# Output projection's weights scaled and split on GpSimd instead of ScalarE and VectorE, in a one-core decoder layer

## The chip, the cores and the metric

The kernel runs on one core of a Trainium2 chip. The metric is the device time of one execution in microseconds (us), taken as the median of three runs. A core has a matrix engine (TensorE, PE in the profile, with its weight loads as PEld), VectorE (DVE), ScalarE (ACT), GpSimd (POOL) and SyncE (SP). Each engine works through its own list of instructions in order, and waits at an instruction until what it needs has arrived. All transfers to and from memory in this kernel are issued from SP's list, in order as well.

## The reference, cut to what matters

One layer over 2048 tokens of width 1024. Four mixers of width 256 each make a part of `ycat`; each part is normalised; one product with `w_out` follows, and the result is added to `x`:

```python
y_a = _chunked_sgu(a_u, a_v, sgu_w[l], sgu_b[l])
y_b = _multiscale_pool(b_in, pool_w[l], pool_scale[l])
y_c = _swa_sink_attention(c_q, c_k, c_v, swa_sinks[l], rel_bias)
y_d = _stick_breaking_attention(d_q, d_k, d_v)
ycat = jnp.stack([y_a, y_b, y_c, y_d], axis=2)
ycat = _rmsnorm(ycat, mix_out_gain[l].reshape(N_MIXERS, GROUP_WIDTH))
x = x + ycat.reshape(B, S, D_MODEL) @ w_out[l]
h = _rmsnorm(x, norm_ffn[l])
gate, up = jnp.split(h @ w_gate_up[l], 2, axis=-1)
x = x + (jax.nn.silu(gate) * up) @ w_down[l]
```

## The kernel before, in words

Every product is made of three passes of TensorE on split operands: a number is rounded to a high part, and the low part is what the rounding left over. So each weight matrix is loaded, scaled, rounded (high part) and subtracted (low part) before it can be used. For `w_out` the function `load_wo` does this. It takes the matrix in eight pieces k = 0 to 7 of 128 rows. Piece k is loaded into a buffer `oraw` (128x1024, 512 KB; two such buffers, so the load of piece k waits until piece k-2 has been read), and gives two pairs `wo` (128x512 high and low each), one for each half n of the output's columns. `gout` holds the gains by which the rows are scaled.

The program has three stages that matter here. In the first, `stick` works through eight chunks of the stick-breaking attention (pair 0 and 1, c = 0 to 3). Each of its steps goes around the engines: `z` (PE), two sigmoids `tfix` and `s` (ACT), a running product `pr` (DVE), `s` times `pr` (line 343: DVE, but GpSimd for i = 3 of the last chunk, by `ON_G`), transposes `tr` (PE), `wt` high (ACT) and low (DVE), and the product `acc` (PE). The last chunk ends with `accs`, `yp` and `ysb`, and SP stores `ysb` into `yd`, two stores.

`mixer_c` is the sliding-window attention, in eight steps s of 256 tokens (`swa`). Step s loads `kr` and, for two groups, `qr`; GpSimd rounds `qr` into `cq` (line 460) and subtracts (line 461); PE makes the logits `z` (line 468); then come a maximum, exponentials on ACT (line 490), transposes `trc` (line 504), copies of these into the buffer `block` (line 506, ACT), the products `o` (line 510) and a store into `yd`. Its steps run beside the last chunk of `stick`, and then beside the output projection.

In `last()` the pieces of `w_out` are prepared beside the last chunk of `stick` and the first steps of `swa`. Then comes `out_proj`, over 16 row blocks b of 128 tokens: load `y` from `yd`; four sums of squares `junk` (ACT); `orr` (a power, on GpSimd, line 149); scale `y`; transpose to `yT` (high on ACT, low on DVE); for each half 8 x 3 products `ops` with `wo` (lines 728 to 730, 48 for a row block); add to `xres`. `finish` normalises the result, transposes it (line 690) and stores it; its power `fr` is also on GpSimd. After that come the feed-forward stages, to the end of the program.

Which instruction stands where in each engine's list is set by the framework's scheduling at build time (`schedule_with_timeline_sim`), from the order in the code, the data that each needs, the buffers and its own costs for the operations. So a change of one function moves others' instructions too. On the chip the lists are fixed.

Of the kernel before, what the change touches and what calls it, by code (L numbers as in the profile page):

```python
# [9 lines left out]
F32 = mybir.dt.float32  # L10
F32R = mybir.dt.float32r
AF = mybir.ActivationFunctionType
ALU = mybir.AluOpType
# [103 lines left out]
def _build(nc, tc, A, top):  # L117
    V, S, G = nc.vector, nc.scalar, nc.gpsimd

    def load(out, in_):  # L120
        nc.sync.dma_start(out, in_)
# [40 lines left out]
    def fetch(pool, f):  # L162

        tag, n = ("k4", 16) if f else ("raw", 2)
        raw = [pool.tile([P, 2, CH], F32, name="fraw", tag=tag, bufs=n) for _ in range(2)]
        for u in range(2):
            load(raw[u], A["w_gu"][f, :, u].rearrange("p (a k) m -> p a (k m)", a=2))
        return raw

    with ExitStack() as ph1:  # L170
# [462 lines left out]
        def load_wo():  # L633

            gout = ring[0].tile([P, KT], F32, name="gout", bufs=1)
            load(gout, A["mix_out_gain"])
            for k in range(KT):
                raw = ring[0].tile([P, 2, CH], F32, name="oraw", tag="raw", bufs=2)
                load(raw, A["w_out"][k * P:(k + 1) * P, :].rearrange("p (n c) -> p n c", n=2))
                wo.append([ring[0].tile([P, 2, CH], F32R, name="wo", tag="k4") for _ in range(2)])  # L640
                for n, w in enumerate(wo[-1]):
                    S.activation(w[:, 0], raw[:, n], AF.Copy, scale=gout[:, k:k + 1])
                    V.scalar_tensor_tensor(w[:, 1], raw[:, n], gout[:, k:k + 1], w[:, 0].bitcast(F32),
                                           op0=ALU.mult, op1=ALU.subtract)
                yield

        def split_T(src, dst, banks=(("tr", 2), ("tr", 2))):
# [267 lines left out]
        def last():  # L915

            yield from upto(99)
            fps.close()
            ring.append(top.enter_context(tc.tile_pool(name="ring", bufs=16, side="right", reuse_waits="tile")))
            for _ in load_wo():  # L920
                yield 0.5
            while done[0] < 2:
                yield next(sw[0])
# [39 lines left out]
    with ExitStack() as ph4:  # L963
# [149 lines left out]
        for blk in range(T // TB):  # L1113
            for f in range(NF):
                raw = first if blk + f == 0 else fetch(ring, f)
# [18 lines left out]
```

## Time and profile before

| | us |
|---|---|
| median of 3 runs (2399.28 to 2400.28) | 2400.15 |
| the profiled execution's own time | 2402.21 |
| its span, from first to last instruction | 2400.5 |
| PE busy in the span | 2271.7 (95%) |
| DVE busy | 1505.8 (63%) |
| ACT busy | 1024.8 (43%) |
| POOL busy | 278.8 (12%) |

The profiled execution was 2.06 us above the median, and 1.71 us of it lie outside the span. Busy shares are means over the whole program; the stage in question is less than a tenth of it. A row of the timeline gives the start in us from the span's beginning, the duration of the group in us, engine, line, operation, output and inputs, the number of instructions (x1, x2), and in brackets the idle time before it with what ended it. PEclk is the granted TensorE clock as a share of 2.4 GHz.

### The profile page before, as it was taken

How to read it: one execution, taken by the hardware profiler on the slowest of the kernel's cores; microseconds unless marked ns; L12 is line 12 of the kernel's file. 1: busy time of each engine (PE TensorE's matmuls, PEld its weight loads, DVE VectorE, ACT ScalarE, POOL GpSimd, SP SyncE). 2: the span in 40 equal slices, each digit the busy share in tenths (PEclk: the TensorE clock that was granted, in tenths of full speed). 3: DMA queues.
4: the chain of work that ended last, by engine and by line, in shares of the span. 5: the costliest groups of instructions: out<-in, count | busy, mean ns of one | idle time of the engine just before them, and what ended most of it. 6: DMA issues, size and time to landing. Idle time of an engine off the chain costs nothing.

```text
span 2400.5 us, 31011 instructions
## 1 busy us (share of the span) xinstructions
PE 2271.7 (95%) x11432; PEld 1915.6 (80%) x11432; DVE 1505.8 (63%) x2467; ACT 1024.8 (43%) x2176; POOL 278.8 (12%) x356
## 2 busy tenths in 40 slices
PE   6999999998977899989999999999999999999998
PEld 6989888887865787768888888888888888888886
DVE  4356989887675455567666666644576666653443
ACT  5556656664455243343333333533333333333332
POOL 4222423441122120100000000000000000000000
PEclk9999999998977999999999999999999999999999
DMA  7534322333532245753222223665432222234553
GB/s 278 190 130 171 139 89 88 106 103 112 192 105 91 100 139 162 234 186 98 91 92 80 79 79 125 200 201 168 146 104 84 79 86 89 87 107 141 186 174 123
DMA packets 141001, 314.05 MB, mean 131 GB/s; under 512 B 12688, under 2 KB 68400, under 8 KB 134704
## 3 DMA queue, kind: packets, MB, share of 16 engines
q1 hardware_dynamic: 140848, 312.06, 38.8%
q8 instruction: 90, 1.47, 0.2%
q14 instruction: 63, 0.52, 0.1%
HBM read 229.44 MB, written 82.58 MB: 130 GB/s over the span
## 4 chain that ended last, share of the span: by engine, by line
PE 73%; DMA 10%; DVE 8%; ACT 4%; issue 3%; POOL 2%; SPq 1%; DVEq 0%; POOLq 0%; ACTq 0%
PE dn L1081 20%; PE gb L1025 15%; PE gc L1025 10%; PE ga L1025 10%; DVE pr L338 2%; PE ops L728 2%; PE ops L730 2%; PE ops L729 2%; DMA y<-yd 1%; DVE s L343 1%; DMA qr<-cd 1%; DMA xt<-in_x 1%; PE ps L277 1%; PE ps L278 1%; PE ps L279 1%
## 5 line engine op out<-in xcount | busy, mean ns | idle before, releaser
L1081 PE MATMUL dn<-wd,act 128*128 128x512 f32 x2112 | 479.5, 389 | 0.0
L1081 PEld LDWEIGHTS dn<-wd,act 128*128 128x128 f32 x2112 | 396.5, 188 | 82.4
L1025 PE MATMUL gb<-T,fw 128*128 128x512 f32 x1584 | 388.2, 394 | 0.0
L1025 PEld LDWEIGHTS gb<-T,fw 128*128 128x128 f32 x1584 | 297.5, 188 | 68.5
L1025 PE MATMUL ga<-B,fw 128*128 128x512 f32 x1056 | 259.5, 394 | 0.0
L1012 ACT CAST fw<-fsum 128x512 fp32r<-128x512 f32 x176 | 108.4, 619 | 308.4 <-DVE fsum L1008 162.3
L1025 PEld LDWEIGHTS ga<-B,fw 128*128 128x128 f32 x1056 | 198.6, 188 | 45.9
L975 DVE TENSOR_TENSOR wd<-wr,wd 128x512 fp32r<-128x512 f32 x176 | 115.2, 689 | 186.4 <-ACT wd L1075 186.2
L1075 ACT CAST wd<-wr 128x512 fp32r<-128x512 f32 x176 | 102.0, 619 | 236.5 <-DMA wr<-in_w_down 208.8
L149 POOL TENSOR_TENSOR fr<-rs_t,mhalf 128x1 f32<-128x1 f32 x32 | 21.5, 674 | 1433.1 <-DVE rs_t L148 1428.2
L975 DVE TENSOR_TENSOR fw<-fsum,fw 128x512 fp32r<-128x512 f32 x176 | 120.9, 690 | 36.4 <-ACT fw L1012 36.0
L1025 PE MATMUL gc<-T,fw 128*128 128x512 f32 x528 | 131.6, 397 | 5.8 <-DVE T L975 5.8
L338 DVE TENSOR_TENSOR_SCAN pr<-tfix,cr 128x513 f32<-128x513 f32 x96 | 126.1, 1323 | 11.4 <-ACT tfix L329 11.1
L1025 PE MATMUL gc<-B,fw 128*128 128x512 f32 x528 | 128.0, 391 | 0.0
L1025 PEld LDWEIGHTS gc<-T,fw 128*128 128x128 f32 x528 | 100.6, 191 | 28.7 <-DVE T L975 6.2
L728 PE MATMUL ops<-wo,yT 128*128 128x512 f32 x256 | 105.7, 413 | 11.5 <-ACT yT L656 10.8
L1025 PEld LDWEIGHTS gc<-B,fw 128*128 128x128 f32 x528 | 99.2, 188 | 21.7
L343 DVE TENSOR_TENSOR s<-s,pr 128x512 f32<-128x512 f32 (+3 forms) x152 | 107.9, 717 | 10.8 <-POOL s L335 4.5
L356 DVE TENSOR_TENSOR wt<-tr,wt 128x512 fp32r<-128x512 f32 (+3 forms) x160 | 94.1, 601 | 29.5 <-ACT wt L355 29.3
L1012 ACT CAST fw<-fraw 128x512 fp32r<-128x512 f32 x132 | 81.7, 621 | 66.9 <-DVE fw L975 32.4
L730 PE MATMUL ops<-wo,yT 128*128 128x512 f32 x256 | 102.7, 407 | 3.4 <-DVE yT L657 3.4
L729 PE MATMUL ops<-wo,yT 128*128 128x512 f32 x256 | 104.2, 408 | 0.0
(234 smaller groups left out, 4499.0 us busy)
## 6 DMA issues: line engine op xcount, KB each, us to landing
fraw<-in_w_gu SPq DMA_DIRECT2D x88, 512.0 KB
wr<-in_w_down SPq DMA_DIRECT2D x88, 512.0 KB
h<-hd SPq DMA_DIRECT2D x32, 1024.0 KB
actd<-up SPq DMA_DIRECT2D x88, 256.0 KB
ar<-actd SPq DMA_DIRECT2D x88, 256.0 KB
hd<-h SPq DMA_DIRECT2D x16, 1024.0 KB
xr<-in_xT SPq DMA_DIRECT2D x16, 512.0 KB
xt<-in_x SPq DMA_DIRECT2D x16, 512.0 KB
```

Of the source, the lines that this page charges most:

```text
L277: nc.tensor.matmul(o, hk[:, 0], w(k, 0), start=k == 0, stop=False)
L338: V.tensor_tensor_scan(pr[:, c0:][:, ::-1], t[:, c0:][:, ::-1], t[:, c0:][:, ::-1], carry[h][i], op0=ALU.mult, op1=ALU.bypass)
L343: (G if (4 * pair + c, i) in ON_G else V).tensor_tensor(w[:, c0:], w[:, c0:], pr[:, c0 + 1:], op=ALU.mult)
L356: V.tensor_tensor(wt[:, 1, r], tr[:, r], wt[:, 0, r].bitcast(F32), op=ALU.subtract)
L728: nc.tensor.matmul(ps, yk[:, 0, :], wo[k][half][:, 0], start=k == 0, stop=False)
L729: nc.tensor.matmul(ps, yk[:, 0, :], wo[k][half][:, 1], start=False, stop=False)
L730: nc.tensor.matmul(ps, yk[:, 1, :], wo[k][half][:, 0], start=False, stop=k == KT - 1)
L975: V.tensor_tensor(dst, src, hi.bitcast(F32), op=ALU.subtract)
L1012: S.copy(w[:, 0], src)
L1025: nc.tensor.matmul(bank, w[:, wi, sl], hc[n][:, k, hi], start=start and k + wi + hi == 0, stop=stop and k == 3 and wi == 1, skip_group_che ...
L1075: S.copy(w[n][:, 0], wr[:, n])
L1081: nc.tensor.matmul(pss[2 * i + n], a[:, ai, t], w[n][:, wi], start=f + ai + wi == 0, stop=f == NF - 1 and ai == 1)
```

## The change

High and low part of every piece of `wo` came from one instruction on ACT (scale and round) and one on DVE (scale and subtract). Now GpSimd scales `oraw` in place, rounds it, and subtracts. Two instructions a half-piece become three, so 16 on ACT and 16 on DVE become 48 on GpSimd.

```diff
@@ load_wo
                 load(raw, A["w_out"][k * P:(k + 1) * P, :].rearrange("p (n c) -> p n c", n=2))
                 wo.append([ring[0].tile([P, 2, CH], F32R, name="wo", tag="k4") for _ in range(2)])
                 for n, w in enumerate(wo[-1]):
-                    S.activation(w[:, 0], raw[:, n], AF.Copy, scale=gout[:, k:k + 1])
-                    V.scalar_tensor_tensor(w[:, 1], raw[:, n], gout[:, k:k + 1], w[:, 0].bitcast(F32),
-                                           op0=ALU.mult, op1=ALU.subtract)
+                    G.tensor_scalar(raw[:, n], raw[:, n], gout[:, k:k + 1], None, op0=ALU.mult)
+                    G.tensor_copy(w[:, 0], raw[:, n])
+                    G.tensor_tensor(w[:, 1], raw[:, n], w[:, 0].bitcast(F32), op=ALU.subtract)
                 yield
```

The lists of the engines change far beyond these lines, from the place where piece 0 arrives to the end of the output projection.

On ACT, in the last chunk of `stick`, this is what stood and stands behind the copy of `kr` for step 2 of `swa` (a minus is the list before, a plus the list now, a blank both):

```order
 L450 CAST ck<-kr 128x2x256
 L506 COPY block<-trc 128x2x128
-L642 ACTIVATE wo<-oraw,gout 128x512 x2
-L506 COPY block<-trc 128x512
-L642 ACTIVATE wo<-oraw,gout 128x512 x2
-L355 CAST wt<-tr 128x256
-L342 COPY cr<-pr 128x1
-L329 ACTIVATE tfix_222<-z 128x512
```

Pieces 2 and 3 stood here between the steps of `stick`; now nothing in ACT's list waits for `oraw` at all.

On SP, around the two stores of `ysb` that end `stick` (yd_66 and yd_67; vd_69 holds values for `swa`, and y<-yd_60 are the first rows of the output projection), the list now reads:

```order
 L121 DMA yd_66<-ysb 128x2x128
+L121 DMA oraw<-in_w_out 128x1024
 L121 DMA yd_67<-ysb 128x2x128
+L121 DMA kr<-cd_189 128x1x256 x2
+L121 DMA block<-vd_69 128x128
 L121 DMA gffn<-in_norm_ffn 128x8
 L121 DMA y<-yd_60 128x1024
+L121 DMA oraw<-in_w_out 128x1024
 L121 DMA xres<-in_x 128x1024
```

The loads of pieces 4 and 5, which stood with all others ahead of this place, are now behind the store, and a load into `block` stands ahead of the first `y`. Pieces 6 and 7 are loaded later still, behind the loads of `qr` for step 4 and of `kr` for step 5.

On GpSimd the end of the weight preparation, pieces 6 and 7, now stands in this order (none of it but the lines 460 and 461 was there before):

```order
+L644 TENSOR_TENSOR wo<-oraw,wo 128x512
+L642 TENSOR_SCALAR oraw<-oraw,gout 128x512 x2
+L460 CAST cq<-qr 128x256 x2
+L643 CAST wo<-oraw 128x512
+L642 TENSOR_SCALAR oraw<-oraw,gout 128x512 x2
+L643 CAST wo<-oraw 128x512
+L461 TENSOR_TENSOR cq<-qr,cq 128x256 x2
+L644 TENSOR_TENSOR wo<-oraw,wo 128x512
+L643 CAST wo<-oraw 128x512 x2
+L644 TENSOR_TENSOR wo<-oraw,wo 128x512
+L460 CAST cq<-qr 128x256 x2
+L644 TENSOR_TENSOR wo<-oraw,wo 128x512 x2
```

Piece 7's low parts are the last two instructions, behind roundings of `cq` for a later step of `swa`.

## Rows read from the trace of the kernel before

**Rows 1.** Busy time by stretch; core 0, then length, busy us and counts, PEclk, DMA.

```profile
672.00:761.00 89.00, 59.26 (x290) 47.48 (x289) 66.91 (x98) 59.59 (x144) 24.82 (x36) 0.76 0.27 87
761.00:791.00 30.00, 24.82 (x110) 21.34 (x111) 9.17 (x24) 9.99 (x33) 3.02 (x3) 0.69 0.35 121
791.00:1062.00 271.00, 246.18 (x1290) 203.00 (x1288) 138.99 (x282) 102.81 (x281) 36.16 (x53) 0.96 0.54 177
1062.00:2400.00 1338.00, 1325.30 (x5771) 1085.49 (x5771) 808.70 (x1265) 464.01 (x834) 12.11 (x16) 1.00 0.36 119
```

**Rows 2.** Waits of ACT, 672 to 761 us: total us, times, longest.

```profile
ACT wo L642 <- DMA oraw<-in_w_out: 11.0, 3, 5.7
```

**Rows 3.** Chain that ended last, 660 to 860 us: shares by line.

```profile
by line: DMA y<-yd 10.4%; DMA qr<-cd 8.4%; PE ops L728 8.4%; DMA oraw<-in_w_out 8.3%; PE ops L729 7.9%; PE ops L730 7.5%; PE o L510 6.0%; PE z L468 3.4%; PE trc L504 3.0%; issue 3.0%; POOL cq L461 2.7%; ACT junk L671 2.6%; ACT wo L642 2.4%;
```

**Rows 4.** Instructions on `wo`: durations in ns (min/median/max), first and last start.

```profile
L642 ACT ACTIVATE wo<-oraw,gout x16: 706/722/745, 677.5 to 727.2; 128x512 fp32r<-128x512 f32 x16
L643 DVE SCALAR_TENSOR_TENSOR wo<-oraw,gout,wo x16: 702/743/891, 680.1 to 731.8; 128x512 fp32r<-128x512 f32 x16
```

**Rows 5.** Timeline of ACT: a wait for `oraw`, the end of `stick`, first `y`.

```profile
696.91 1.33 ACT L642 ACTIVATE wo<-oraw,gout 128x512 fp32r<-128x512 f32 x2 [5.65 <-DMA oraw<-in_w_out]
...
760.66 0.37 ACT L376 COPY ysb<-yp 128x256 f32<-128x256 f32 x1 [1.79 <-PE yp L374]
...
769.60 0.42 ACT L671 ACTIVATE junk<-y 128x256 f32<-128x256 f32 x1 [5.91 <-DMA y<-yd]
```

**Rows 6.** Timeline of PE: `stick`, step 2 of `swa`, and the first row blocks.

```profile
698.56 0.58 PE L364 MATMUL acc<-wt,vstack 128*128 128x256 f32 x1 [5.69 <-ACT wt L355]
...
750.81 1.65 PE L468 MATMUL z<-ck,cq 128*128 128x256 f32 x6 [3.13 <-POOL cq L461]
...
770.63 1.97 PE L510 MATMUL o<-block 128*128 128x64 f32 x8 [4.07 <-ACT block L506]
772.39 1.06 PE L504 MATMUL trc<-ident,block 128*128 128x128 f32 x4
...
777.87 0.78 PE L728 MATMUL ops<-wo,yT 128*128 128x512 f32 x1
...
791.90 0.40 PE L728 MATMUL ops<-wo,yT 128*128 128x512 f32 x1
...
832.38 0.79 PE L728 MATMUL ops<-wo,yT 128*128 128x512 f32 x1 [7.31 <-ACT yT L656]
```

**Rows 7.** GpSimd by line and shape, whole span: busy us, mean ns; idle before.

```profile
L461 POOL TENSOR_TENSOR cq<-qr,cq 128x256 fp32r<-128x256 f32 x32 | 26.0, 832 | 0.2
...
L149 POOL TENSOR_TENSOR orr<-rs_t,mhalf 128x4 f32<-128x4 f32 x16 | 16.7, 1042 | 105.2 <-DVE rs_t L148 105.2
...
L460 POOL CAST cq<-qr 128x256 fp32r<-128x256 f32 x32 | 14.5, 461 | 127.1 <-DMA qr<-cd 66.9 <-PE z L468 56.6 <-issue 3.5
...
L343 POOL TENSOR_TENSOR s<-s,pr 128x512 f32<-128x512 f32 x8 | 9.6, 1197 | 63.5 <-DVE pr L338 50.0 <-PE trc L504 13.5
...
L252 POOL TENSOR_TENSOR w_k<-wraw,w_k 128x1024 fp32r<-128x1024 f32 x1 | 2.4, 2397 | 5.8 <-ACT w_k L251 5.8
...
L526 POOL TENSOR_SCALAR_AFFINE_SELECT sgw<-sgw 128x512 f32<-128x512 f32 x1 | 0.9, 938 | 7.6 <-DMA sgw<-in_sgu_wT 7.6
```

**Rows 8.** Timeline of GpSimd: one instruction beside a busy DVE.

```profile
692.54 1.92 POOL L343 TENSOR_TENSOR s<-s,pr 128x512 f32<-128x512 f32 x1 [2.43 <-DVE pr L338]
```

**Rows 9.** Timeline of DVE: one instruction twice, beside GpSimd and alone.

```profile
693.61 1.41 DVE L451 TENSOR_TENSOR ck<-kr,ck 64x512 fp32r<-64x512 f32 x1
...
745.88 0.69 DVE L451 TENSOR_TENSOR ck<-kr,ck 64x512 fp32r<-64x512 f32 x1
```

**Rows 10.** Timeline of SP's queue: loads of pieces 0 and 1, and the end of `stick`.

```profile
672.61 0.92 SPq L121 DMA_DIRECT2D oraw<-in_w_out  x2
...
761.06 1.04 SPq L121 DMA_DIRECT2D yd<-ysb  x2
...
762.88 0.43 SPq L121 DMA_DIRECT2D y<-yd  x1
```

## Prediction

> **What bounds the kernel now.** I read the stretches first. PE is busy for 246.18 of the 271.00 us from the second row block of the output projection to the feed-forward stages, and for 1325.30 of the 1338.00 us after that; but from 672 to 761 us, where the weights are prepared, only for 59.26 of 89.00 us, at a granted clock of 0.76 [rows 1]. So in this stretch PE is not the bound, and all that happens before the feed-forward stages moves the end by the same amount, since behind them PE hardly waits. What the reader is to see there is a loop around the engines: DVE is busy for 66.91 us, ACT for 59.59, and each stick-breaking step has to go through both.
>
> The waits of ACT come next: it stood 11.0 us, in three waits, before the scaling of `wo`, because `oraw` had not arrived [rows 2]. The longest, 5.65 us, holds up everything behind it in ACT's list [rows 5], and PE's wait of 5.69 us for a `wt` that stands there shows the stick-breaking loop hanging on it [rows 6]. The chain that ended last says the same: over 200 us, 8.3% are `oraw` loads and 2.4% ACT on `wo` [rows 3]. So ACT's part of the preparation is on the path. The preparation's result is not: the last DVE instruction on `wo` started at 731.8 us [rows 4], and the first product that needs it at 777.87 [rows 6].
>
> I call the moment at which SP issues the store of the last `ysb`, 761.06 us [rows 10], the store point. The sum goes by two pieces: how much earlier the store point comes, and how much later, measured from it, the second row block starts: before, at 791.90 [rows 6], 30.8 us behind the store point.
>
> **What the change removes.** ACT loses 16 x 0.72 = 11.6 us of work and DVE 16 x 0.743 = 11.9 us [rows 4], and ACT no longer waits for `oraw`. On the path were the waits, 11.0 us [rows 2], and of the work what the chain holds of it, 2.4% of 200 us = 4.8 us [rows 3]; the rest lies beside the waits. That makes 15.8 us. The most it could be is the waits and all of DVE's work, 22.9 us. The least: GpSimd's new work slows DVE's instructions that read two inputs from SBUF. L451 took 1.41 us beside a GpSimd instruction, and 0.69 alone [rows 9]; the GpSimd instruction beside it took 1.92 us where the mean is 1.20 [rows 7, 8]. At the 9 multiplications and 2 L451 that DVE still has to do in this chunk, with 0.7 us added to each, 7.7 of the 15.8 us are lost, 8.1 remain. I take 16 us: until the store point GpSimd has only pieces 0 to 3, most of them while DVE is at scans and at subtractions from PSUM. The store point comes to 745.
>
> The Trainium skill (GPSIMD Engine Reference, section 1, Specifications) says that GpSimd's way into SBUF is shared with VectorE, and that they contend where a VectorE instruction has two SBUF inputs. The two durations of L451 agree with it. Were it to hit every scan as hard as L451, no gain would be left before the store point; by the bound above 8.1 us are left.
>
> **What the change adds, on GpSimd.** It had nothing of this size of each kind. A subtraction of 128x512 lies between L343, 1.20 us, and half of the 128x1024 one, 2.397 / 2 = 1.20 us [rows 7]: 1.2. The rounding is twice L460: 2 x 0.46 = 0.92 at most, since an instruction has a fixed part; I take 0.8. The scaling has one tensor input; between the rounding and L526, 0.94 us [rows 7]: I take 0.9. That is 2.9 us for a half-piece, 46 us for all 16, where GpSimd was busy for 24.82 of 89 us [rows 1]. Before the store point this fits: pieces 0 to 3 are 8 x 2.9 = 23 us.
>
> **Where it goes wrong: pieces 4 to 7.** In the lists (shown with the change) the loads of pieces 4 and 5 stand behind the store point, 6 and 7 further on. So half of the preparation, which was done 30 us before the store point, starts only there, and it sits on one engine that also makes `cq` and the powers. Counted from the store point:
>
> - Piece 4's load lands after 5 us: pieces 0 and 1 were issued at 672.61 [rows 10] and used from 677.5 [rows 4].
> - From there to piece 7's last low part GpSimd's list has 8 x 2.9 = 23.2 us on `wo`, 6 roundings of 0.46 and 6 subtractions of 0.83 for `cq`, and 3 powers of 1.04 [rows 7]: 2.8 + 5.0 + 3.1. Together 34 us.
> - It also waits. SP may not issue the first `y` and piece 5 until a load into `block` in front of them is free, and this hangs on the products `o` of step 2. Before, these ended at 770.63 + 1.97 = 772.6, of which 4.07 us were a wait for ACT that now goes away [rows 6]; so about 8 us behind the store point, and 2 us more for the `z` of step 3 that PE now has between them: 10. Then `y` needs 6.7 us to land (762.88 to 769.60 [rows 5, 10]), and four sums of squares before the power that stands in the middle of piece 5. GpSimd stands there from 5 + 2 x 0.9 + 2 x 0.83 + 0.8 = 9 to about 18, but for the scaling of piece 5: 7 us. The loads of pieces 6 and 7 wait for the buffers of 4 and 5, and the `qr` of step 5 for those of step 4; I put 4 us on these.
>
> 5 + 34 + 11 = 50, and 1 us for PE: the second row block starts 51 us behind the store point, 20 us later than the 30.8 of before. Bounds: without any wait 39 (8 later); with GpSimd's 34 us stretched by 1.4 (1.92 to 1.20 would be 1.6, but DVE was busy for only 0.3 of 761 to 791 us [rows 1]) 64 (33 later).
>
> **What is given back.** While PE waits for `wo` it does work that was done later before. Counted in the two lists up to the second row block: 11 `z` of line 468, 20 transposes of line 504, 20 products of line 510 more. At the low clock of these stretches they took 1.65 / 6, 1.06 / 4 and 1.97 / 8 us each [rows 6], that is 3.0 + 5.3 + 4.9 = 13.2 us, half of it at the full clock at which they would else run: 6.6, I take 6. It also brings `swa` ahead of the row blocks, whose wait of 7.31 us before 832.38 [rows 6] came from a `y` late in SP's list. Now the third block waits about 3 us for its `y`: 4 us back. Against that the clock: PE has been mostly idle, and at 0.69 in the stretch before the row blocks [rows 1]; some us at the lower level when they start cost 2. Later stretches are left as they are.
>
> **The sum.** -16 + 20 - 6 - 4 + 2 = -4 us. The profiled execution was 2402.21, so 2398; it was 2.06 above the median, so the median comes to 2396. With each of the two large terms moved to its bounds alone (8.1 to 22.9, 8 to 33) it goes from 2384 to 2409; as the case's own range I take 2388 to 2404.
>
> **Rivals.** *The weights come too late*: GpSimd's tail becomes the bound of the start of the projection. The place is the last low part of piece 7; the price is each us by which it falls beyond 55 us behind the store point, the point at which the sum turns to zero. At the bound of 64 us the kernel is 9 us slower, at 2409; with loads as slow as two of those before (the chain's 8.3% of 200 us are 16.6 for `oraw` [rows 3]) 2414. For it: GpSimd's instructions grew under load [rows 8], and all sits in series. Against it: DVE has little to do there. The same page of the Trainium skill (section 4.1, Engine selection) puts elementwise work on VectorE and calls GpSimd about 2x slower with two inputs. The rows give 1.2 us against 0.74 on DVE [rows 4, 7], 1.6x. By the page's factor a subtraction would be 1.5 us, the 8 behind the store point 2.3 us more, and the sum -2.
>
> *The tail is hidden*: the waits for `y` and for the loads fall away, the block starts 41 us behind the store point, and most of the gain of the first stretch stays: -14, 2386. For it: PE has the work of two steps of `swa` to do meanwhile. Against it: the order on SP.
>
> *Nothing happens before the store point*: the loop is held by DVE, at 66.91 of 89 us, and by its waits for one another, so that only 8 us are gained: +4, 2404. Against it: the chain runs through `oraw` and ACT.
>
> **Chances.** The forecast 0.5, the late weights 0.25, the hidden tail 0.17, the first stretch without gain 0.08. This kernel's measurement can tell 0.2%, 4.8 us, from no change: the forecast's own spread puts 0.22 of its 0.5 beyond it as faster, 0.24 within and 0.04 slower. With the rivals: faster 0.22 + 0.17 = 0.39, within 0.24 + 0.05 = 0.29, slower 0.04 + 0.25 + 0.03 = 0.32. The range takes in the hidden tail and most of the late weights: 2384 to 2412.
>
> **What would show it.** ACT without a wait for `oraw`, and `ysb` stored near 745 us. `oraw` of piece 4 issued right behind it. GpSimd standing some 9 us at the first power. The last low part about 50 us behind the store, and the second row block right behind that, near 796. Fewer us lost before the fourth row block. Wrong would be a GpSimd subtraction much above 1.2 us, a store point later than 752, or a gap of PE of more than 10 us where the row blocks start.

## The result, and the profile after

The changed kernel takes 2424.45 us (median of 4 runs, 2421.46 to 2427.09) against 2400.11 us of before on the same chip (4 runs): a ratio of 1.0100, 95% interval 1.0085 to 1.0115. It is 24 us slower, where 2396 was forecast and 2412 was the upper end of the range. The profiled execution took 2423.01 us with a span of 2421.3, 20.8 us more than before.

The same four stretches as in [rows 1], for the changed kernel (us, then busy time of PE, PE's weight loads, DVE, ACT and GpSimd, the granted clock, DMA):

```profile
672.00:761.00 89.00, 63.14 (x317) 51.66 (x316) 56.50 (x73) 47.75 (x113) 53.94 (x55) 0.74 0.24 75
761.00:791.00 30.00, 16.92 (x78) 14.32 (x78) 13.40 (x30) 13.95 (x48) 18.26 (x18) 0.63 0.42 145
791.00:1062.00 271.00, 238.51 (x1210) 195.44 (x1209) 132.49 (x267) 90.19 (x263) 49.10 (x66) 0.93 0.46 152
1062.00:2400.00 1338.00, 1332.33 (x5812) 1091.22 (x5811) 808.71 (x1263) 471.23 (x835) 10.55 (x13) 1.00 0.37 122
```

As forecast, DVE and ACT have 10 to 12 us less to do from 672 to 761 us, and GpSimd has 54 us in place of 25. But from 761 to 791 us PE is busy for 16.92 us in place of 24.82, at a granted clock of 0.63 in place of 0.69. In the feed-forward stages nothing is lost. The last product of the output projection starts at 1070.43 us, at 1048.94 before: 21.5 us, the whole loss, lie ahead of these stages.

SP's queue around the store point (start, time for issuing, what is loaded or stored), to be read against [rows 10]:

```profile
750.48 0.36 SPq L121 DMA_DIRECT2D yd<-ysb  x1
750.93 0.42 SPq L121 DMA_DIRECT2D oraw<-in_w_out  x1
...
756.17 0.42 SPq L121 DMA_DIRECT2D y<-yd  x1
756.69 0.38 SPq L121 DMA_DIRECT2D oraw<-in_w_out  x1
...
780.28 0.35 SPq L121 DMA_DIRECT2D oraw<-in_w_out  x1
...
784.19 1.38 SPq L121 DMA_DIRECT2D oraw<-in_w_out  x1
```

The store point came at 750.48: 10.6 us earlier than before, where 16 were forecast. The loads of pieces 4 to 7 stand behind it, as the lists said. Now GpSimd in the stretch that follows (start, us, what; in brackets how long it stood before and for whom):

```profile
753.35 0.40 POOL L460 CAST cq<-qr 128x256 fp32r<-128x256 f32 x1 [14.55 <-PE z L468]
...
755.15 3.11 POOL L642 TENSOR_SCALAR oraw<-oraw,gout 128x512 f32<-128x512 f32 x2 [0.76 <-DMA oraw<-in_w_out]
...
765.21 3.13 POOL L642 TENSOR_SCALAR oraw<-oraw,gout 128x512 f32<-128x512 f32 x2 [5.01 <-DMA oraw<-in_w_out]
768.31 1.03 POOL L149 TENSOR_TENSOR orr<-rs_t,mhalf 128x4 f32<-128x4 f32 x1
...
792.85 0.76 POOL L460 CAST cq<-qr 128x256 fp32r<-128x256 f32 x2 [5.23 <-PE z L468]
793.55 0.62 POOL L643 CAST wo<-oraw 128x512 fp32r<-128x512 f32 x1
794.15 3.11 POOL L642 TENSOR_SCALAR oraw<-oraw,gout 128x512 f32<-128x512 f32 x2
...
804.77 0.40 POOL L460 CAST cq<-qr 128x256 fp32r<-128x256 f32 x1 [1.94 <-DMA qr<-cd]
807.72 0.40 POOL L460 CAST cq<-qr 128x256 fp32r<-128x256 f32 x1 [2.55 <-DMA qr<-cd]
808.08 2.50 POOL L644 TENSOR_TENSOR wo<-oraw,wo 128x512 fp32r<-128x512 f32 x2
```

The last low parts end at 810.58, 60 us behind the store point (forecast: 50). Two scalings take 3.1 us where 1.8 were reckoned, and casts of `cq`, which stand among the weights in the same list, make the weights wait for `z` (5.2 us before 792.85) and for loads of `qr`. What PE makes of it, to be read against [rows 6]:

```profile
774.52 1.18 PE L504 MATMUL trc<-ident,block 128*128 128x128 f32 x4 [12.05 <-ACT block L490]
...
780.90 0.78 PE L728 MATMUL ops<-wo,yT 128*128 128x512 f32 x1
...
809.40 0.79 PE L729 MATMUL ops<-wo,yT 128*128 128x512 f32 x1 [2.14 <-POOL wo L644]
...
814.42 0.39 PE L728 MATMUL ops<-wo,yT 128*128 128x512 f32 x1
...
857.12 0.80 PE L728 MATMUL ops<-wo,yT 128*128 128x512 f32 x1 [9.88 <-ACT yT L656]
```

The first block's products start only 3 us later than before. The second row block starts at 814.42, 63.9 us behind the store point, where 51 were forecast. In the kernel before it starts at 791.20, with the 49th product; the 791.90 of the prediction is the 52nd:

```profile
791.20 0.39 PE L728 MATMUL ops<-wo,yT 128*128 128x512 f32 x1
```

That is 30.1 us behind the store point, not 30.8, and the changed kernel is 23.2 us later there. Before the fourth row block PE waits 9.88 us, in place of 7.31; that wait was to shrink.

The ledger in the prediction's terms: store point -10.6 (forecast -16), from there to the second row block +33.8 (63.9 - 30.1; forecast +20), from there to the last product -1.7 (forecast -6 - 4 + 2 = -8). The sum is +21.5 where -4 stood. All three terms failed to the same side.

The third term, in the columns of [rows 1], from the second row block to the projection's end, first of before, then of the changed kernel:

```profile
791.20:1049.30 258.10, 236.46 (x1244) 195.35 (x1243) 134.13 (x274) 94.18 (x270) 35.62 (x52) 0.96 0.51 167
814.40:1070.80 256.40, 229.72 (x1173) 189.44 (x1172) 130.35 (x262) 86.72 (x247) 34.49 (x48) 0.95 0.50 166
```

PE is busy for 6.7 us less, which is the 6 us given back; but it stands for 26.7 us in place of 21.6, 5 us more, where 4 us less were forecast.

### The profile page after: what moved, and what is told of

Its sections match the earlier page's. It is cut to its first block, busy times and chain, and to the rows that moved or that the text cites. A ratio compares the mean times of both kernels' runs of the same rounds, so it can differ in the third digit from the quotient of the medians.

```text
span 2421.3 us, 31029 instructions
## 1 busy us (share of the span) xinstructions
PE 2279.9 (94%) x11432; PEld 1921.9 (79%) x11432; DVE 1503.3 (62%) x2451; ACT 1016.8 (42%) x2160; POOL 336.0 (14%) x404
## 4 chain that ended last, share of the span: by engine, by line
PE 61%; DMA 3%; DVE 1%; ACT 1%; issue 0%; SPq 0%; POOL 0%; DVEq 0%; ACTq 0%; POOLq 0%
PE dn L1081 20%; PE gb L1025 15%; PE gc L1025 10%; PE ga L1025 10%; PE ops L728 2%; PE ops L729 2%; PE ops L730 2%; DMA y<-yd 1%; PE ytr L690 0%; PE o L510 0%; DMA b<-hTd 0%; ACT junk L671 0%; DMA fraw<-in_w_gu 0%; DMA x2d<-xres 0%; DMA hsd<-b 0%
## 5 line engine op out<-in xcount | busy, mean ns | idle before, releaser
L728 PE MATMUL ops<-wo,yT 128*128 128x512 f32 x256 | 107.5, 420 | 19.6 <-ACT yT L656 19.4
L343 DVE TENSOR_TENSOR s<-s,pr 128x512 f32<-128x512 f32 (+3 forms) x152 | 107.0, 711 | 11.2 <-POOL s L335 4.4
L729 PE MATMUL ops<-wo,yT 128*128 128x512 f32 x256 | 107.0, 418 | 3.7 <-POOL wo L644 3.7
L353 PE MATMUL tr<-ident,s 128*128 128x128 f32 x544 | 96.5, 283 | 10.8 <-DVE wt L356 6.9
```

What stands on the lines that cost most here:

```text
L343: (G if (4 * pair + c, i) in ON_G else V).tensor_tensor(w[:, c0:], w[:, c0:], pr[:, c0 + 1:], op=ALU.mult)
L353: nc.tensor.transpose(tr[:, i * P:(i + 1) * P], wq[i][:, col:col + P], ident)
L728: nc.tensor.matmul(ps, yk[:, 0, :], wo[k][half][:, 0], start=k == 0, stop=False)
L729: nc.tensor.matmul(ps, yk[:, 0, :], wo[k][half][:, 1], start=False, stop=False)
```

## The experiments

The runs were made on four chips in turn, each beside runs of the kernel before on the same chip, whose medians there were 2399.72, 2403.59, 2403.50 and 2404.49 us. So the kernels are compared by their ratio to before; "by ratio" is 2400.11 times it, the scale in which the expectations are written. Marks in a profile carry the chip's offset too: in four_y_before, which lays this path out nearly as before, they come 1.6 to 3.2 us later than in before. The columns: products `z` of `swa` on PE from 600 us to the store point, the store point, the start of the second row block (the 49th product of L728 to L730), and the end of the projection's last product.

| kernel | ratio, 95% interval | by ratio | `z` ahead | store point | 2nd row block | projection's end |
|---|---|---|---|---|---|---|
| before | 1 | 2400.1 | 56 | 761.06 | 791.2 | 1049.3 |
| changed | 1.0100 (1.0085 to 1.0115) | 2424.1 | 34 | 750.48 | 814.4 | 1070.8 |
| early_on_gpsimd | 1.0024 (1.0015 to 1.0033) | 2405.9 | 34 | 751.84 | 790.2 | 1053.0 |
| late_on_gpsimd | 1.0041 (1.0029 to 1.0053) | 2410.0 | 40 | 754.96 | 789.4 | 1062.6 |
| no_scaling | 1.0006 (0.9996 to 1.0017) | 2401.6 | 38 | 746.14 | 789.1 | 1052.0 |
| broadcast_scaling | 1.0048 (1.0036 to 1.0060) | 2411.6 | 40 | 747.21 | 790.8 | 1059.6 |
| swa_sooner_after | 1.0046 (1.0034 to 1.0059) | 2411.2 | 45 | 755.66 | 802.1 | 1064.3 |
| five_buffers | 1.0029 (1.0019 to 1.0038) | 2407.1 | 26 | 739.76 | 783.5 | 1056.6 |
| before_five_buffers | 1.0032 (1.0021 to 1.0044) | 2407.8 | 56 | 758.95 | 790.2 | 1052.6 |
| swa_later | 0.9989 (0.9980 to 0.9998) | 2397.5 | 24 | 732.97 | 784.4 | 1050.5 |
| swa_some_later | 1.0014 (1.0006 to 1.0023) | 2403.5 | 44 | 748.87 | 796.6 | 1053.9 |
| y_by_act_queue_before | 1.0031 (1.0020 to 1.0042) | 2407.6 | 56 | 759.80 | 790.7 | 1057.6 |
| y_by_act_queue_after | 1.0081 (1.0068 to 1.0095) | 2419.6 | 34 | 753.59 | 820.1 | 1077.7 |
| four_y_before | 1.0003 (0.9995 to 1.0012) | 2400.8 | 56 | 763.16 | 792.8 | 1052.5 |
| four_y_after | 1.0112 (1.0097 to 1.0126) | 2427.0 | 34 | 753.39 | 811.0 | 1079.2 |
| four_y_five_oraw | 1.0008 (1.0000 to 1.0017) | 2402.0 | 26 | 740.74 | 783.6 | 1053.2 |

Line numbers shift by a few in kernels with added lines.

### Which pieces cost the time

**early_on_gpsimd.** In `load_wo`, half of the pieces go back to ScalarE and VectorE:

```diff
                 for n, w in enumerate(wo[-1]):
+                    if k >= 4:
+                        S.activation(w[:, 0], raw[:, n], AF.Copy, scale=gout[:, k:k + 1])
+                        V.scalar_tensor_tensor(w[:, 1], raw[:, n], gout[:, k:k + 1], w[:, 0].bitcast(F32),
+                                               op0=ALU.mult, op1=ALU.subtract)
+                        continue
                     G.tensor_scalar(raw[:, n], raw[:, n], gout[:, k:k + 1], None, op0=ALU.mult)
```

> Pieces 0 to 3 on GpSimd, pieces 4 to 7 as before; in SP's list the loads of pieces 4 to 7 stand behind the store point, as in the changed kernel. Theory T: the tail behind the store point loses GpSimd's 29 us, and ScalarE and VectorE, idle there, take 1.5 us for a half-piece: second row block about 42 us behind the store point, 2400 to 2408. Rival O: the loads are as late as in the changed kernel, the block starts 55 us or more behind the store point, 2415 to 2424. Rival C: half of the loss, about 2412.

2405.9 by ratio, with the second row block 38 us behind the store point. The loads of pieces 4 to 7 still stand behind the store point; SP's queue around it and ACT's half-pieces of three of these pieces show it:

```profile
751.84 0.36 SPq L121 DMA_DIRECT2D yd<-ysb  x1
752.29 0.42 SPq L121 DMA_DIRECT2D oraw<-in_w_out  x1
...
757.72 0.38 SPq L121 DMA_DIRECT2D oraw<-in_w_out  x1
```

```profile
756.14 1.34 ACT L643 ACTIVATE wo<-oraw,gout 128x512 fp32r<-128x512 f32 x2 [2.10 <-DMA oraw<-in_w_out]
766.71 1.32 ACT L643 ACTIVATE wo<-oraw,gout 128x512 fp32r<-128x512 f32 x2
...
779.93 1.34 ACT L643 ACTIVATE wo<-oraw,gout 128x512 fp32r<-128x512 f32 x2 [4.68 <-DMA oraw<-in_w_out]
```

Theory T's ranges hold, those of O and C do not: with GpSimd's work ahead of the store point the same, 18 of the 24 us are back once the late pieces are off GpSimd. The other 6 are left; of the change, only the four early pieces are then on GpSimd, and which step of theirs costs it stays open. Not all loads are as late, though. Those of pieces 4 and 5 are issued 0.5 and 5.9 us behind the store point (0.5 and 6.2 in the changed kernel), those of 6 and 7 at 7.8 and 20.4 us (29.8 and 33.7). Ahead of the load of piece 6 the changed kernel's SP stood for a subtraction on GpSimd, which had to give the buffer back (774 to 790 us; waited for: us in total, times, longest):

```profile
SPq L121 <- POOL wo L644: 5.9, 1, 5.9
```

So GpSimd's pace makes the late loads later still. SP's order around them changed as well, and the run does not take the two apart.

**late_on_gpsimd.** The same edit with `k < 4`.

> Pieces 0 to 3 are prepared as before (ScalarE, VectorE), pieces 4 to 7 on GpSimd; in SP's list all eight loads then stand ahead of the store point. Theory T (the loss is GpSimd's work on pieces 4 to 7, which begins only behind the store point and stands in series there): GpSimd's 8 x 3.6 us now begin before the store point, some 10 us of them are left behind it, the second row block starts about 40 us behind the store point in place of 63, time 2400 to 2408. Rival O (the loss is the late loads in SP's queue, whichever engine prepares): nothing is late any more, 31 us behind the store point, 2392 to 2400. Rival C (GpSimd's instructions slow VectorE's through the shared way into SBUF, all along): half of the instructions, half of the loss, about 2412.

2410.0 by ratio, above T's range, and above O's 2400 although no load is late any more. It is near C's 2412, but C wants the same from either half of the pieces, and the run before lost only 6 us. The second row block starts 34 us behind the store point, in time; the loss comes later, at the sixth row block:

```profile
878.70 0.79 PE L733 MATMUL ops<-wo,yT 128*128 128x512 f32 x1 [11.86 <-ACT yT L661]
```

That is a wait for `y`, as at 857.12 in the changed kernel. It was not foreseen, and the runs on `y` below try it.

**no_scaling.** The line of `G.tensor_scalar` is deleted.

> The changed kernel with the scaling by the gain left out (wo is split from the unscaled w_out): GpSimd has 16 x 1.6 = 25.8 us less, 12.9 of them behind the store point. Theory T (the loss is GpSimd's tail behind the store point): second row block 48 to 51 us behind the store point in place of 64, time 2408 to 2414. Rival O (what is late is the loads and SP's order, and early_on_gpsimd came out well only because of ScalarE and VectorE's other order): within 5 us of the changed kernel, 2418 to 2424.

2401.6 by ratio: better than T's range. The block starts 43 us behind the store point (T: 48 to 51). The 25.8 us less on GpSimd bring back 22 us, more than their half behind the store point, and the lists change with them: seven of the eight loads of `oraw` now stand ahead of the store point, in place of four. So O's range is missed, but the run does not separate GpSimd's seconds from late loads.

**broadcast_scaling**, suggested by the durations below:

```diff
-                    G.tensor_scalar(raw[:, n], raw[:, n], gout[:, k:k + 1], None, op0=ALU.mult)
+                    G.tensor_tensor(raw[:, n], raw[:, n], gout[:, k:k + 1].broadcast_to([P, CH]), op=ALU.mult)
```

> The changed kernel with the scaling as a tensor_tensor with the gain's column broadcast along the row (1.16 us for a half-piece in scaling_forms) in place of tensor_scalar (1.61): the same result from GpSimd with 16 x 0.45 = 7.2 us less, 3.6 of them behind the store point. Theory T (GpSimd's tail sets the start of the second row block): 4 to 8 us come back, 2416 to 2421. A rival, that the order that the scheduler makes of it matters more than this: outside that, 2405 to 2415 or above 2424.

2411.6 by ratio: 12 us came back, more than the 4 to 8 of T, so the rival of the other order has its part: six of the eight loads now stand ahead of the store point, and the second row block starts 44 us behind it. GpSimd's seconds and the places of the loads were not separated here.

**swa_sooner_after.** One number of the changed kernel, `ratios[7]`, 2.20 to 4.00:

> The changed kernel with the ratio 4.00: everything on GpSimd, but in SP's list seven of the eight loads of oraw stand ahead of the store point in place of four; swa is as far as in the changed kernel. Theory T (GpSimd's tail behind the store point): about half of the tail is done before it, the second row block starts 40 to 50 us behind the store point in place of 64; of the 24 us lost 8 to 16 come back, 2408 to 2416. Rival, that the weights on GpSimd cost the same wherever they stand: 2420 to 2428.

2411.2 by ratio and the second row block 46 us behind the store point, both within T's ranges: the same work on GpSimd costs about half as much when more of it is issued ahead of the store point. Two of its premises did not hold: six of the eight loads stand ahead of the store point, not seven, and `swa` is not as far as in the changed kernel, with 45 products `z` ahead in place of 34.

### Was the gain ahead of the store point one?

**five_buffers** (the changed kernel) and **before_five_buffers** (the kernel before) take `oraw` from five buffers, two of the old tag and three of a pool of their own, which is open during the last stick chunk:

```diff
-                raw = ring[0].tile([P, 2, CH], F32, name="oraw", tag="raw", bufs=2)
+                raw = (ring if k % 5 < 2 else rawp)[0].tile([P, 2, CH], F32, name="oraw", tag="raw",
+                                                               bufs=2 if k % 5 < 2 else 3)
```

> The kernel before, with five buffers for oraw in place of two: ScalarE's 11 us of waits for oraw go, nothing moves to GpSimd. If the waits of ScalarE are on the path, as the prediction has it, the store point comes 8 to 11 us earlier (750 to 753) and the time is 2388 to 2394. The rival, that the loop around VectorE and ScalarE holds this stretch whatever the waits are: store point within 4 us of 761, 2396 to 2402.

Its ACT from 670 to 761 us (waited for: us in total, times, longest):

```profile
ACT ck L450 <- PE z L468: 5.4, 1, 5.4
ACT es L486 <- DVE es L484: 5.2, 1, 5.2
ACT wo L643 <- DMA oraw<-in_w_out: 4.0, 2, 3.4
```

```profile
758.95 3.55 SPq L121 DMA_DIRECT2D yd<-ysb  x2
```

ACT's waits for `oraw` fell from 11.0 us [rows 2] to 4.0, and the store point came 2.1 us earlier, not 8 to 11. Counted from the first load of `oraw` (670.29 here, 672.61 before), it did not move at all: 88.7 us in place of 88.5, with as many products `z` ahead of it. Two waits, for `z` and for DVE, stand in place of the one for `oraw`. So ACT's waits for `oraw` do not set the length of this stretch; the rival's store point holds. That the loop around DVE and ACT sets it is the reading that is left, and is not shown. The time, 2407.8 by ratio, is 8 us above before and outside the rival's range too; why stays open.

> All eight pieces on GpSimd as in the changed kernel, but with five buffers for oraw in place of two, so that five loads are issued at once and all eight ahead of the store point. Theory T: GpSimd has 16 x 3.6 = 58 us on wo and some 12 us on cq from about 678 us, without a wait for loads: done near 755, within 10 us of the store point; second row block 35 to 42 us behind it, 2395 to 2406. Rival O: 31 us behind, with the store point at 750: 2388 to 2394. Rival C: nothing is won by the buffers, 2415 to 2425.

Its store point came at 739.76, 21 us earlier than before, and its second row block 8 us earlier, 44 us behind the store point (T: 35 to 42); its projection ends 7 us later than before, and the time is 2407.1 by ratio, a little above T's range. Where the lead is gone is seen in PE's row of the third row block:

```profile
809.13 0.80 PE L729 MATMUL ops<-wo,yT 128*128 128x512 f32 x1 [8.92 <-ACT yT L657]
```

That called for a look at what else had moved. PE's lines of `swa` up to the store point, first of before (672.6 to 761.06 us), then of the changed kernel (672.5 to 750.48; xcount, then busy us and mean ns, then idle time before them):

```profile
L468 PE MATMUL z<-ck,cq 128*128 128x256 f32 x56 | 12.6, 355 | 5.6 <-POOL cq L461 3.1 <-DVE block L470 2.2
```

```profile
L468 PE MATMUL z<-ck,cq 128*128 128x256 f32 x34 | 7.5, 323 | 3.7 <-DVE block L516 3.7
```

22 products `z` moved from ahead of the store point to behind it; in five_buffers it is 30. (Of the transposes `trc` and the products `o` as many stand ahead of it in the changed kernel as before, 36 and 56.) An earlier store point is then partly work put off. **swa_later** moves such work alone, in the kernel before, with nothing on GpSimd:

```diff
-        ratios = (38 / 10.8, 38 / 21.6, 38 / 32.4, 52 / 43.2, 4.00, 1.20, 1.00, 2.20)
+        ratios = (38 / 10.8, 38 / 21.6, 38 / 32.4, 52 / 43.2, 4.00, 1.20, 1.00, 1.20)
```

> The kernel before with the ratio of the last chunk 1.20 in place of 2.20: nothing goes to GpSimd, but most of swa's work moves from ahead of the store point to behind it. Theory D (an earlier store point is bought with swa's work, which PE, DVE and ScalarE must do all the same): store point 15 us or more earlier, 65 to 74 us behind the first load of oraw in place of 88, and the time not lower, 2400 to 2430. Rival F (the feed-forward starts earlier by what the store point is earlier): 2380 to 2392.

```profile
732.97 0.89 SPq L121 DMA_DIRECT2D yd<-ysb  x2
```

The store point came 28 us earlier, with 32 products `z`, 32 `trc` and all 56 `o` moved behind it, more than in the changed kernel. The projection ends 1.2 us later in the trace (its chip runs the kernel before some 4 us slower). The time is 2397.5 by ratio, 2.6 us less than before: within the 0.2% that the prediction took for no change, though its interval ends below 1. That is 2.5 us below D's range and 5.5 above F's 2380 to 2392. D is the nearer, and its point stands: 28 us at the mark are worth 2.6 at the end. The expected 65 to 74 us behind the first load of `oraw` were a poor mark: it is 42, since that load came later too. It is the one kernel of the table whose interval lies below 1.

**swa_some_later**, the same number at 1.60:

> The kernel before with the ratio 1.60: a little of swa's work moves behind the store point (4 of 36 transposes of the probabilities up to the end of the sticks, in the list). Theory D: store point 2 to 8 us earlier, time 2398 to 2408. Rival F: 2393 to 2398.

2403.5 by ratio, in D's range and outside F's, with the store point 12 us earlier, more than D said.

### What GpSimd's instructions cost

**scaling_forms** has four forms of the first step, each for two pieces, two of which do not scale:

```diff
+                    if k % 4 == 0:
                         G.tensor_scalar(raw[:, n], raw[:, n], gout[:, k:k + 1], None, op0=ALU.mult)
+                    elif k % 4 == 1:
+                        G.tensor_scalar(raw[:, n], raw[:, n], 1.0, None, op0=ALU.mult)
+                    elif k % 4 == 2:
+                        G.tensor_tensor(raw[:, n], raw[:, n], gout[:, k:k + 1].broadcast_to([P, CH]), op=ALU.mult)
+                    else:
+                        G.tensor_copy(raw[:, n], raw[:, n])
```

> The changed kernel with four forms in place of the scaling, each for two of the eight pieces: tensor_scalar by the gain's column as changed (1.61 us for 128x512); tensor_scalar by the constant 1.0; tensor_tensor by the gain's column broadcast along the row; a plain copy in place. The last is no scaling, nor is the second. Theory P (the column operand makes it dear): constant 0.6 to 0.9, broadcast 1.2 to 1.3. Rival G (every tensor_scalar of GpSimd costs this, whatever the operand): constant 1.5 to 1.65, broadcast 1.2 to 1.3. Rival N (VectorE's load on the shared way to SBUF stretched it): durations that fall where VectorE stands.

By line and shape (xcount, then busy us and mean ns, then idle time before them):

```profile
L643 POOL TENSOR_SCALAR oraw<-oraw,gout 128x512 f32<-128x512 f32 x4 | 6.7, 1674 | 0.5 <-DMA oraw<-in_w_out 0.5
L645 POOL TENSOR_SCALAR oraw<-oraw 128x512 f32<-128x512 f32 x4 | 5.9, 1492 | 3.0 <-DMA oraw<-in_w_out 3.0
L647 POOL TENSOR_TENSOR oraw<-oraw,gout 128x512 f32<-128x512 f32 x4 | 4.6, 1164 | 4.0 <-DMA oraw<-in_w_out 4.0
L649 POOL COPY oraw<-oraw 128x512 f32<-128x512 f32 x4 | 3.4, 874 | 0.0
```

Rival G holds, its ranges missed by no more than 0.04 us: `tensor_scalar` is the dear form whatever its operand, dearer than the operation with two tensors. (In broadcast_scaling all 16 of the two-tensor form took 1.27 us in the mean.) Rival N falls with the changed kernel's rows: 1.61 us over all 16 scalings, 1.59 over the 8 behind the store point, where DVE has little to do.

### Does `y` hold the later row blocks?

The waits at 857.12 (changed) and 832.38 (before [rows 6]) are for ACT's copies `yT`, which stand in ACT's list behind the sums of squares of the next block's `y`. Two tries were made to take `y` out of the way.

**y_by_act_queue_before** and **y_by_act_queue_after**, in `rows(b)`: `S.dma_start(y, ...)` in place of `load(y, ...)`.

> The kernel before with the loads of y issued by ScalarE's DMA queue in place of SP's. Theory Q: the wait of 7.3 us before the fourth row block goes, 2390 to 2396. Rival B: the waits stay, 2397 to 2404.

> The changed kernel with the loads of y issued by ScalarE's DMA queue in place of SP's. Theory Q (behind the second row block the end is set by y, which stands in SP's list behind the loads of kr, qr and block): the wait of 9.9 us before the fourth row block goes, 2408 to 2416. Rival B (y waits for its buffer and for the work of swa, not for the queue): the waits stay, 2419 to 2428; a wait of ScalarE for y's buffer may add to it.

2407.6 and 2419.6 by ratio. The waits shrank (4.2 us in place of 7.3 before the fourth block of the first; 3.9 in place of 9.9 in the second), but others grew (5.6 us at the sixth block of the first, 8.7 us for the last `wo` in the second). Theory Q fails on before, where B's range (to 2404) is missed as well; on the changed kernel the gain of 5 us is at B's edge.

**four_y_before**, **four_y_after**, **four_y_five_oraw**: `bufs=4` for `y` in place of 3, in the kernel before, in the changed one and in five_buffers.

> The kernel before with four buffers for y in place of three. Theory L (behind the second row block the row blocks run in a loop: the copies yT of block b stand in ScalarE's list behind the sums of squares of block b+1, which wait 8 to 10 us for y's load, which waits for the buffer that block b-2 gives back): the wait of 7.3 us before the fourth row block and the smaller ones go, 2385 to 2395. Rival W (the steps of swa set when these blocks can start, the buffer matters not): 2396 to 2404.

> The changed kernel with four buffers for y. Theory L: the wait of 9.9 us before the fourth row block goes, GpSimd's tail before the second one stays: 2408 to 2416. Rival W: 2420 to 2428.

> All pieces on GpSimd, five buffers for oraw and four for y: store point and second row block early, as in five_buffers (68 and 112 us behind the first load of oraw). Theory L: with the loop of y open the early start reaches the end, 2388 to 2397. Rival W: block 4 still starts near 830 us whatever comes before it, 2403 to 2410.

2400.8, 2427.0 and 2402.0 by ratio: W's ranges for the first two; with five buffers for `oraw` it gave 5 us, in neither range. Theory L's forecasts fail, but four_y_before did not open the loop that L names. SP issues four `y` at once in place of three, and each later load is for one block further. The fourth block's sums of squares are done at 783 us, in place of 806. Its copies `yT`, though, now stand in ACT's list behind the sums of squares of the sixth block, and these wait for the sixth `y`, issued at 820.99:

```profile
769.90 0.96 SPq L121 DMA_DIRECT2D y<-yd  x2
...
831.68 0.42 ACT L671 ACTIVATE junk<-y 128x256 f32<-128x256 f32 x1 [10.44 <-DMA y<-yd]
...
833.72 1.05 ACT L656 CAST yT<-ytr 128x512 fp32r<-128x512 f32 x2
...
834.33 0.79 PE L728 MATMUL ops<-wo,yT 128*128 128x512 f32 x1 [7.77 <-ACT yT L656]
```

And the buffer does hold `y`: in both kernels SP stands 5.0 us, up to 800.08 before and 801.71 here, until the last transposes of the first row block have read the buffer that the next `y` takes (four_y_before, 790 to 850 us):

```profile
SPq L121 <- PE ytr L690: 8.4, 2, 5.0
```

So a fourth buffer moved ACT's list on by a block and left the wait; whether the buffer, SP's order or ACT's order sets the pace of these blocks stays open. In the eleven kernels of the table whose second row block starts between 783 and 793 us, the sixth one starts between 870 and 879 us, with store points from 733 to 763.

## Why the prediction was wrong, point by point

**ACT's waits for `oraw` on the path: wrong.** "On the path were the waits, 11.0 us" is the first step that failed. before_five_buffers takes 7 of the 11 us away and moves the store point by 2.1 us, and not at all against the first load of `oraw`; in place of the wait that went ACT has two others, of 5.4 and 5.2 us, for PE and DVE. The rival *Nothing happens before the store point* had named this, at 0.08; its argument against, that the chain runs through `oraw` and ACT, was the mistake: the chain shows which wait came last, not that the next one is shorter.

**The store point at 745, and that it moves the end: wrong.** It came to 750.48, and 22 products `z` that stood ahead of it stand behind it now. The step "all that happens before the feed-forward stages moves the end by the same amount" was applied to a mark and not to all the work: swa_later shifts that mark by 28 us and the time by 2.6. The prediction had counted what `swa` does up to the second row block and booked 6 us as given back. PE has indeed 6.7 us less to do from there (with 40 products `o` more ahead of it, not the 20 counted); but the 22 products `z` were not counted against the earlier store point.

**The slowing of DVE by GpSimd: there, and small.** From 672 to 761 us the scans of 128x513 took 1.301 us before and 1.448 after (12 each), the 128x512 multiplications of L343 0.772 and 0.902 (9 each): 12 x 0.147 + 9 x 0.130 = 2.9 us, where the bound was 7.7. It falls on a few of them: seven of the 12 scans kept 1.27 to 1.29 us, and the one at 696 us, beside GpSimd's subtractions, took 2.36.

**GpSimd's half-piece, 2.9 us: it took 3.6.** Scaling 1.61 (0.9 reckoned), rounding 0.68 (0.8), subtraction 1.33 (1.2). The scaling, for having one tensor input, had been put between the rounding and L526, a select of 128x512; scaling_forms shows it above the two-tensor operation of the same size. The Trainium skill (GPSIMD Engine Reference, section 4.1, Engine selection) says that an operation with one input runs at roughly line rate on GpSimd and one with two at about half of VectorE's speed. For the subtraction the trace agrees: 1.33 us to 0.74 on DVE [rows 4] is 1.8x. For the scaling it does not: the one-input 1.61 us lie above the two-input 1.33.

**The second row block 51 us behind the store point: 64.** The right mechanism, mis-sized. Behind the store point GpSimd was busy for 37.3 us up to the last low part (34 reckoned; the 8 scalings alone are 12.7 in place of 7.2) and stood for 60.1 - 37.3 = 22.8 (16 reckoned): 8.3 for `z`, 8.4 for `qr` and 6.0 for `oraw`. (The first line counts 11.7 us from ahead of the store point as well.)

```profile
POOL cq L460 <- PE z L468: 20.0, 3, 14.6
POOL cq L460 <- DMA qr<-cd: 8.4, 4, 2.5
POOL oraw L642 <- DMA oraw<-in_w_out: 6.0, 3, 5.0
```

What was missed above all is the 5.23 us at 792.85: a cast of `cq` waits for the `z` before it, and pieces 6 and 7 wait behind the cast. PE added 3.8 us, where 1 was reckoned. The first power came at 17.8, as reckoned (18), but by luck: `y` was issued 5.7 us behind the store point, not 10, and the power then stood behind piece 5's scaling. The rival *The weights come too late* had 64 us at its bound, and the block started there; its time of 2409 was too low because it kept the 16 us of gain and the 8 given back.

**4 us fewer waiting for `y`: wrong.** The fourth block's copies `yT` stand behind the sums of squares of the fifth block, whose `y` was issued at 844.17, behind a `kr` that held SP for 3.96 us. PE waited 9.88 us instead of 7.31, and 5 us more in all from the second row block on.

What was right: ACT without waits for `oraw`, the four loads behind the store point, no loss in the feed-forward stages, and the sign of the ledger's three terms. Of the signs of being wrong that the prediction named, one came: PE's gap of 12.05 us before 774.52, ahead of the row blocks. Of the 24 us, early_on_gpsimd puts some 18 on pieces 4 to 7 on GpSimd, with the loads that this holds up, and 6 on the rest.

## What to carry to other kernels

A wait on the last chain is worth only what the next wait in the same loop leaves of it; take it away alone (here by more buffers) before its length is booked as a gain. Where a scheduler fills a stretch with other work, an earlier end of the stretch says nothing until the work done in it is counted too. Work moved to an idle engine is paid for at that engine's rate and with what stands between it in the list: look where its last piece is needed, and price each instruction from a row of the same form.

## Not expected of the hardware

On GpSimd a `tensor_scalar` of 128x512 took 1.49 us (constant operand) to 1.67 (column operand), a `tensor_tensor` with the column broadcast 1.16 to 1.27, a copy from f32 to f32 0.87 and a rounding copy to fp32r 0.61 (median) to 0.70 (mean). The form with one tensor input is dearer than the one with two.
